# Low parts of some down-projection chunks by an accumulating transfer, with other rates for the modulation rows and fewer idle products at the start

## The chip, the cores and the metric

The kernel runs on one core of a Trainium2 chip, in one launch. The metric is the device time of one execution in microseconds (us); less is better. Each kernel was executed several times, and one execution was recorded by the hardware profiler.

## What is computed

Two layers of an encoder over 512 tokens of width 1024, in float32. Each layer has three sub-layers: a SwiGLU block with 2816 hidden features, a mixer (two attentions, a pooling branch, gates, an output projection), and a second SwiGLU block. Ahead of each stands an RMS norm with a shift and a scale, behind it a gate; these come from a vector `c` through the matrix `w_ada`.

```python
c_act = silu(c)
for l in range(2):
    mod = (c_act @ w_ada[l] + b_ada[l]).reshape(B, 9, 1024)
    h = rms_norm(x, gain[l, 0]) * (1 + mod[:, 1]) + mod[:, 0]
    x = x + 0.5 * mod[:, 2] * ((silu(h @ w_gate) * (h @ w_up)) @ w_down)
    h = rms_norm(x, gain[l, 1]) * (1 + mod[:, 4]) + mod[:, 3]
    x = x + mod[:, 5] * hybrid_mixer(h, ...)
    h = rms_norm(x, gain[l, 2]) * (1 + mod[:, 7]) + mod[:, 6]
    x = x + 0.5 * mod[:, 8] * ((silu(h @ w_gate2) * (h @ w_up2)) @ w_down2)
```

## The kernel before

**Split products.** Every float32 operand is held as two tiles of the rounded type float32r: a high part (the value rounded) and a low part (value minus high part). A product is three matmuls into one PSUM bank, written in `triple` in the order high x high (L119), one factor's low part (L120), the other's (L121). In the down projections (`k_outer`) the weights are the stationary factor, and L121 is the one that needs the weights' low part, `wlo`; L119 and L120 need only the high part, `whi`. With 512 columns these products start some 0.23 us apart.

**Weight chunks.** `wchunk` fetches one chunk of 512 KB: SyncE issues the load into `raw` (two buffers), ScalarE writes the high part (`nc.scalar.copy(hi, raw)`, L272), VectorE the low part (`raw - hi`, L274). `whi` and `wlo` have three buffers each, so the chunk three places on waits until TensorE has finished with this one.

**The four SwiGLU blocks** (class `Ffn`) are counted in the order of the run: the first and second belong to layer 0, the third and fourth to layer 1; a mixer stands between the first and second and between the third and fourth. Each block takes its 22 hidden tiles in four parts of 6, 6, 4 and 6 (`PARTS`). In a part, the gate and up products are made (mostly in pairs by a Winograd-like scheme, `pair`, with weights split by `pair_weights`, which does not go through `wchunk`), and then two passes of `k_outer` multiply with `w_down`, for output columns 0 to 511 (`c0 == 0`, PSUM banks "acc") and 512 to 1023 (`c0 == T`, banks "mm"). A pass has `nf // 2` chunks: three in parts of 6, two in the part of 4. The last two chunks of a pass are held and multiplied output tile by output tile; a chunk ahead of them is multiplied as it comes. In the second pass of parts 0 to 2, and only there, `k_outer` gets a hook `then`, which fetches and splits the next part's first pair of gate weights. Per block these passes have 3 + 3 + 2 = 8 chunks, 32 in all, in 12 passes: 8 long ones (three chunks, of which two are held) and 4 short ones (two, both held), where each output tile takes six products of the first chunk and then six of the second.

**Rows of `w_ada`.** One element of `mod` per partition comes from one 512 KB tile of 128 rows, called a row here: `mod_step` has SyncE load it (L195, into a "v2" buffer, four of them, or a "raw" one) and VectorE multiply and sum it against `silu(c)` (L198). Rows 0 to 15 are taken in the opening, the other 128 in a fixed order from a queue; row counts in the text count these. They are taken in two ways. `side_work`, called for a chunk in `wchunk`, adds a rate to a credit and takes a row for each whole 1, while fewer than `upto` are taken; `ADA_FFN` gives rate and `upto` by layer, block and part. It does nothing for five chunks behind a pass with a norm, nor for chunks that do not go through `wchunk`, nor in a block's last part, where the rest is demanded. `mod_need` takes at once all rows that the next use needs: 8 ahead of part 0's down passes of the first block, 24 ahead of its last part (for the mixer), 72 ahead of the second block's last part, 80 in part 0 of the third, 96 ahead of the third's last part. In the mixers, rows go at a rate of 2.4 up to 56 (first layer) and 128.

**The order of instructions.** The code states what depends on what, a few orders by hand (`issue_after`), and a clock of product counts (`later`, `poll`) by which small work is strewn between the products. The framework fixes each engine's order when the program is built, from the order of the code and the times at which it expects operands and buffers; on the chip each engine then takes its instructions in that order and waits for what isn't there.

**The opening** (`Ffn.start`). Squares of `x` are folded by VectorE in two halves; TensorE sums each half over the partitions (L751). Between them `spin` issues products of constants that nothing reads (L738): `SPIN[0]` beside the first half, `SPIN[1]` beside the second, `SPIN[2]` while VectorE computes the inverse root (from L758), `SPIN[3]` behind the transposes (L768). Each is a float32 product, which the profile shows as two records.

Of the kernel before, what the change touches and what calls it, by code (L numbers as in the profile page):

```python
# [18 lines left out]
AF = mybir.ActivationFunctionType  # L19
ALU = mybir.AluOpType  # L20
# [3 lines left out]
T = 512  # L24
# [16 lines left out]
def encoder_kernel(tc, xT, c, w_ada, b_ada, gains, w_gate, w_up, w_down, w_qkv, w_f, w_ubg,  # L41
                   qk_gain, rel, fbias, w_pool, pool_scale, w_branch, w_out, inv_cnt, w_first, out):
    nc = tc.nc
# [20 lines left out]
    def st(shape, dt, tag, bufs):  # L64
        return sb.tile(shape, dt, tag=tag, bufs=bufs, name=nm(tag))

    def acc(shape=(P, T)):
        return ps.tile(list(shape), F32, tag="acc", bufs=4, name=nm("acc"))

    def mmt(shape=(P, T)):  # L70
        return ps.tile(list(shape), F32, tag="mm", bufs=4, name=nm("mm"))
# [45 lines left out]
    def triple(o, lh, ll, rh, rl, start, stop, onto=False):  # L117
        poll()
        mm(o, lh, rh, start=start, stop=False, skip_group_check=onto)  # L119
        mm(o, lh, rl, start=False, stop=False, skip_group_check=onto)  # L120
        mm(o, ll, rh, start=False, stop=stop, skip_group_check=onto)  # L121
        pe[0] += 3.0 * max(o.shape[-1], 256) / T
# [56 lines left out]
    @contextlib.contextmanager  # L179
    def after(what):  # L180

        if what in last:
            with tc.issue_after(last[what]):
                yield
        else:
            yield
# [47 lines left out]
    @contextlib.contextmanager  # L234
    def behind(engine):

        if engine in gate:
            with tc.issue_after(gate[engine]):
                yield
        else:  # L240
            yield

    def side_work():
        if mod_ptr[0] < flow["upto"]:
            mod_credit[0] += flow["rate"]
        while mod_credit[0] >= 1.0:
            mod_credit[0] -= 1.0
            mod_pop()

    def wchunk(src, shape, side=True, spare=None, lo_eng=None, home=None):  # L250
        if lo_eng is None:
            lo_share[1] += 1
            lo_eng = nc.gpsimd if lo_share[0] and lo_share[1] % lo_share[0] == 0 else nc.vector
        if quiet[0] > 0:
            quiet[0] -= 1
            if quiet[0] == 0:
                gate.clear()
        elif side and flow["on"] and mod_tag[0] == "v2":
            side_work()
        raw = st([P] + list(shape), F32, *(home or (("b", NB) if spare else ("raw", NRAW))))  # L260
        last["dma"] = nc.sync.dma_start(raw, src).ins
        if spare == "ptb":
            both = st([P, 2] + list(shape), F32R, "ptb", 2)
            hi, lo = both[:, 0], both[:, 1]
        elif spare == "b":
            hi = st([P] + list(shape), F32R, "b", NB)
            lo = st([P] + list(shape), F32R, "b", NB)
        else:
            hi = st([P] + list(shape), F32R, "whi", 3)
            lo = st([P] + list(shape), F32R, "wlo", 3)  # L270
        with behind("scalar"):
            nc.scalar.copy(hi, raw)  # L272
        with behind("vector"):
            last["lo"] = lo_eng.tensor_tensor(lo, raw, hi.bitcast(F32), op=ALU.subtract).ins  # L274
        return hi, lo
# [108 lines left out]
    def k_outer(chunk_src, nch, lhs_rhs, before_last=None, bank=None, then=None):  # L384

        if before_last is None:
            parts, nheld = [(None, slice(0, T), [(bank or acc)() for _ in range(4)])], 2
        else:  # L390
            parts = [(hs, slice(hs * HALF, (hs + 1) * HALF), [b((P, HALF)) for _ in range(4)])
                     for hs, b in enumerate((mmt, acc))]
            nheld = 3

        def go(part, j, chunks):
            _, cols, accs = part
            for c, hi, lo in chunks:
                for kk in range(2):
                    a, b, x, y = lhs_rhs(hi[:, kk, :], lo[:, kk, :], 2 * c + kk, j)
                    triple(accs[j], a, b, x[:, cols], y[:, cols], start=(c == 0 and kk == 0),  # L400
                           stop=(c == nch - 1 and kk == 1))

        held = []
        for c in range(nch):
            if before_last is not None:
                if c == nch - 2:
                    quiet[0] = 8
                    before_last()
                quiet[0] = 8
            hi, lo = wchunk(chunk_src(c), (2, T))  # L410
            if c < nch - nheld:
                for part in parts:
                    for j in range(4):
                        go(part, j, [(c, hi, lo)])
            else:
                held.append((c, hi, lo))
        if then is not None:
            then()
        if before_last is not None:
            quiet[0] = 5  # L420
        for part in parts:
            for j in range(4):
                go(part, j, held[:-2])
            for j in range(4):
                go(part, j, held[-2:])
                yield j, part[0], part[2][j]
# [14 lines left out]
    STEP = 3  # L441
    PARTS = (6, 6, 4, 6)
    UP_FROM = 1
    SPIN = (4, 4, 8, 3)


    class Ffn:
# [4 lines left out]
        def gate_up(self, which, n, **kw):  # L452
            return wchunk((w_gate, w_up)[which][self.l, self.s, n], (KD, P), **kw)
# [207 lines left out]
        def run(self, nxt):  # L661
            l, s, ms = self.l, self.s, self.ms
            mod_tag[0] = "v2"
            f0 = 0
            for part, nf in enumerate(PARTS):
                flow.update(on=True, behind="norm", **ADA_FFN(l, s, part))
                acts = []
                n = 0
# [63 lines left out]
        def start(self):  # L732
# [3 lines left out]
            def spin(operands, n):  # L736
                for z in range(n):
                    mm(acc((P, P)), ones, operands[z % len(operands)][:, :P], start=True, stop=True)  # L738
# [4 lines left out]
            for half in range(2):  # L743
# [3 lines left out]
                for tile_ in four[2:]:  # L747
                    fold = nc.vector.tensor_tensor(ssum, ssum, tile_, op=ALU.add)
                spin(four, SPIN[half])
                for t in range(NT):  # L750
                    last["sum"] = mm(pv[:, t:t + 1], ssum[:, t * P:(t + 1) * P], ones[:, 0:1], start=False,  # L751
                                     stop=half == 1, skip_group_check=True).ins
            spin([ssum], SPIN[2])
            gate["vector"] = fold.ins
# [14 lines left out]
            with after("turn"):  # L769
                spin([dg[:, 3, :]], SPIN[3])  # L770
            pgs = [(acc(), acc()), (acc(), acc()), (mmt(), mmt())]
# [29 lines left out]
            for d in range(KD):  # L801
                if d:
                    w = wchunk(w_first[d], (6, P), side=False, lo_eng=nc.gpsimd if d > 1 else nc.vector)
                    h(d)
                else:
                    raw, hi, lo = (st([P, 6, P], z, t, n) for z, t, n in
                                   ((F32, "raw", NRAW), (F32R, "whi", 3), (F32R, "wlo", 3)))
                    last["dma"] = nc.sync.dma_start(raw, w_first[d]).ins
                    nc.scalar.copy(hi, raw)
                    w = hi, lo  # L810
                    h(d, lambda: nc.vector.tensor_tensor(lo, raw, hi.bitcast(F32), op=ALU.subtract).ins)
                product(d, w)
# [384 lines left out]
    class Mixer:  # L1197
# [10 lines left out]
        def run(self, nxt):  # L1208
# [77 lines left out]
            for c0 in (0, T):  # L1286
                def src(c):
                    return w_out[l, 2 * c * P:(2 * c + 2) * P, c0:c0 + T].rearrange("(k p) c -> p k c", p=P)

                def ops(hi, lo, kt, j):  # L1290
                    return (hi[:, j * P:(j + 1) * P], lo[:, j * P:(j + 1) * P], mh[kt][:, 0, :], mh[kt][:, 1, :])

                if c0 == 0:
                    nxt.prefetch("b")
                for j, hs, o in k_outer(src, 4, ops, nxt.prefetch_weights if c0 else None):
                    d = c0 // P + j
                    residual_tail(d, hs, o, modc[:, l, 5, d:d + 1], nxt)
# [3 lines left out]

    def ADA_FFN(l, s, part):
        if l == 0 and s == 0:
            return {"rate": 1.0 if part == 0 else 0.5, "upto": 24}
        if l == 0:
            return {"rate": 0.6, "upto": 80}
        return {"rate": 0.5, "upto": 96}

    LO_SHARE = 0

# [66 lines left out]
```

## Time and profile before

| | us |
|---|---|
| three runs, median (lowest to highest) | 2395.15 (2393.12 to 2395.19) |
| the profiled execution | 2398.11 |
| its span | 2396.3 |
| TensorE busy (matmuls) | 2365.8 |
| VectorE busy | 1783.8 |
| ScalarE busy | 1166.6 |
| GpSimd busy | 196.9 |
| mean granted TensorE clock | 0.997 |

PE is TensorE, PEld its weight loads, DVE VectorE, ACT ScalarE, POOL GpSimd, SP SyncE; SPq and POOLq rows are transfers that they issue. A row of the order of time gives start and duration in us, engine, line, operation, output and inputs, shape, count, and in brackets how long the engine sat idle before and for whom. A row of waits gives the total, the number and the longest. A row of the transfers' list ends with the median time in us from issue to landing.

### The profile page before, as it was taken

To read this page: it belongs to the slowest core of one execution; us is meant where nothing else is said; L and a number is where in the kernel's file an instruction comes from. 1 tells how busy PE (TensorE), PEld (TensorE's weight loads), DVE (VectorE), ACT (ScalarE), POOL (GpSimd) and SP (SyncE) were. 2 spreads that over 40 slices of the span, in tenths; PEclk is the share of its full clock that TensorE was granted. 3 is DMA by queue.
4 is the path that set the end of the run, shared out by engine and by line. 5 is a ranking of instruction groups with operands and counts; after the bars stand their busy time and mean duration, and the time that the engine had idled before them with its cause. 6 is when DMAs were issued, how large, how long until landed. Compare 5 with 4: busy or idle time off the path is not lost. (4 is left out here: it accounts for less than half of the span.)

```text
span 2396.3 us, 36743 instructions
## 1 busy us (share of the span) xinstructions
PE 2365.8 (99%) x14182; PEld 2096.9 (88%) x14182; DVE 1783.8 (74%) x3213; ACT 1166.6 (49%) x2048; POOL 196.9 (8%) x309
## 2 busy tenths in 40 slices
PE   8999999999999999999999999899999999999999
PEld 6899988788888898999998999888888888989998
DVE  7988776687668477778779778776866784777784
ACT  5354445676532353544554445456765334544452
POOL 2000002122220000000100000120221101000000
PEclk9999999999999999999999999999999999999999
DMA  7634342333367414334325423523233773223132
GB/s 275 217 101 134 113 167 98 91 97 119 116 209 280 155 65 167 97 120 145 132 89 194 139 90 115 185 79 99 95 122 116 252 248 132 89 97 123 63 115 89
DMA packets 118484, 325.19 MB, mean 136 GB/s; under 512 B 12034, under 2 KB 14338, under 8 KB 118308
## 3 DMA queue, kind: packets, MB, share of 16 engines
q1 hardware_dynamic: 115106, 314.38, 39.1%
q0 software_dynamic: 3200, 8.46, 1.0%
q8 instruction: 111, 1.82, 0.3%
q14 instruction: 65, 0.53, 0.1%
q10 hardware_dynamic: 2, 0.00, 0.0%
HBM read 316.35 MB, written 6.44 MB: 135 GB/s over the span
## 5 line engine op out<-in xcount | busy, mean ns | idle before, releaser
L272 ACT CAST whi<-raw 128x1024 fp32r<-128x1024 f32 (+1 forms) x260 | 270.4, 1044 | 336.7 <-PE acc L120 193.0
L274 DVE TENSOR_TENSOR wlo<-raw,whi 128x1024 fp32r<-128x1024 f32 (+1 forms) x254 | 311.5, 1230 | 142.2 <-ACT whi L272 140.3
L121 PE MATMUL acc<-b,wlo 128*128 128x512 f32 (+1 forms) x704 | 261.8, 373 | 8.4 <-DVE wlo L274 8.4
L119 PE MATMUL acc<-b,whi 128*128 128x512 f32 (+1 forms) x704 | 262.6, 375 | 1.1 <-ACT b L380 1.1
L120 PE MATMUL acc<-b,whi 128*128 128x512 f32 (+1 forms) x704 | 261.5, 372 | 1.2 <-DVE b L381 1.2
L121 PE MATMUL mm<-b,wlo 128*128 128x256 f32 (+1 forms) x768 | 245.8, 320 | 2.0 <-DVE wlo L274 1.9
L119 PE MATMUL mm<-b,whi 128*128 128x256 f32 (+1 forms) x768 | 245.1, 319 | 0.2 <-ACT t L583 0.2
L120 PE MATMUL mm<-b,whi 128*128 128x256 f32 (+1 forms) x768 | 245.2, 319 | 0.0
L198 DVE CUSTOM_DVE_ANT_0 v<-v,b,badac 128x1024 f32<-128x1024 f32 x144 | 186.8, 1306 | 26.8 <-DMA v<-in_w_ada_dram 26.6
L119 PE MATMUL mm<-hhi,whi 128*128 128x256 f32 (+1 forms) x616 | 199.1, 324 | 1.1 <-ACT t L583 1.0
L121 PE MATMUL mm<-hhi,wlo 128*128 128x256 f32 (+1 forms) x616 | 199.1, 323 | 0.5 <-DVE wlo L274 0.5
L120 PE MATMUL mm<-hlo,whi 128*128 128x256 f32 (+1 forms) x616 | 199.1, 323 | 0.0
L120 PE MATMUL acc<-hlo,whi 128*128 128x512 f32 x480 | 188.1, 392 | 1.7 <-DVE hlo L787 1.6
L119 PE MATMUL acc<-hhi,whi 128*128 128x512 f32 x480 | 188.0, 396 | 1.6 <-ACT hhi L784 1.6
L121 PE MATMUL acc<-hhi,wlo 128*128 128x512 f32 x480 | 187.6, 391 | 0.0
L380 ACT CAST whi<-raw 128x1024 fp32r<-128x1024 f32 x96 | 100.6, 1048 | 132.9 <-PE mm L120 79.0
L121 PEld LDWEIGHTS acc<-b,wlo 128*128 128x128 f32 x704 | 133.5, 190 | 32.6 <-DVE wlo L274 9.7
L121 PEld LDWEIGHTS mm<-b,wlo 128*128 128x128 f32 x768 | 147.1, 192 | 13.4 <-DVE wlo L274 3.5
L119 PEld LDWEIGHTS mm<-b,whi 128*128 128x128 f32 x768 | 147.0, 191 | 10.4 <-ACT t L583 0.4
L120 PEld LDWEIGHTS mm<-b,whi 128*128 128x128 f32 x768 | 147.0, 191 | 10.2
L120 PEld LDWEIGHTS acc<-b,whi 128*128 128x128 f32 x704 | 133.4, 190 | 24.6 <-DVE b L381 2.7
L119 PEld LDWEIGHTS acc<-b,whi 128*128 128x128 f32 x704 | 133.4, 190 | 24.3 <-ACT b L380 2.8
(326 smaller groups left out, 6119.0 us busy)
## 6 DMA issues: line engine op xcount, KB each, us to landing
v<-in_w_ada_dram SPq DMA_DIRECT2D x144, 512.0 KB, 5.0
raw<-in_w_down_dram SPq DMA_DIRECT2D x88, 512.0 KB, 3.8
raw<-in_w_up_dram SPq DMA_DIRECT2D x82, 512.0 KB, 3.6
b<-in_w_gate_dram SPq DMA_DIRECT2D x76, 512.0 KB, 6.2
raw<-in_w_ubg_dram SPq DMA_DIRECT2D x56, 512.0 KB, 3.6
raw<-in_w_qkv_dram SPq DMA_DIRECT2D x42, 512.0 KB, 4.0
raw<-in_w_branch_dram SPq DMA_DIRECT2D x24, 512.0 KB, 3.9
raw<-in_w_out_dram SPq DMA_DIRECT2D x16, 512.0 KB, 3.6
```

Of the source, the lines that this page charges most:

```text
L119: mm(o, lh, rh, start=start, stop=False, skip_group_check=onto)
L120: mm(o, lh, rl, start=False, stop=False, skip_group_check=onto)
L121: mm(o, ll, rh, start=False, stop=stop, skip_group_check=onto)
L198: dot = nc.vector.tensor_tensor_reduce(out=raw, in0=raw, in1=silc[0], scale=1.0, scalar=badac[:, l, j, d:d + 1], op0=ALU.mult, op1=ALU.add ...
L272: nc.scalar.copy(hi, raw)
L274: last["lo"] = lo_eng.tensor_tensor(lo, raw, hi.bitcast(F32), op=ALU.subtract).ins
L380: nc.scalar.copy(hi, src)
```

## The change

For the 32 chunks of the passes that have the hook `then`, ScalarE writes a negated copy of the raw tile into the low part's tile (rounded as the high part is), and a transfer of GpSimd's queue reads the same weights again from memory and adds them to it, so the tile holds raw minus high part as before. The rates of the rows change in all blocks. In the opening, four idle products beside the second half and one of the eight behind it are left out.

```diff
-    def wchunk(src, shape, side=True, spare=None, lo_eng=None, home=None):
+    def wchunk(src, shape, side=True, spare=None, lo_eng=None, home=None, by_dma=False):
...
         with behind("scalar"):
             nc.scalar.copy(hi, raw)
+        if by_dma:
+            with behind("scalar"):
+                nc.scalar.activation(lo, raw, AF.Copy, scale=-1.0)
+            nc.gpsimd.dma_start(lo, src, accum_op=ALU.add, max_dma_last_dim=2048)
+            return hi, lo
         with behind("vector"):
             last["lo"] = lo_eng.tensor_tensor(lo, raw, hi.bitcast(F32), op=ALU.subtract).ins
         return hi, lo
...
-            hi, lo = wchunk(chunk_src(c), (2, T))
+            hi, lo = wchunk(chunk_src(c), (2, T), by_dma=then is not None)
...
-    SPIN = (4, 4, 8, 3)
+    SPIN = (4, 0, 7, 3)
...
     def ADA_FFN(l, s, part):
         if l == 0 and s == 0:
-            return {"rate": 1.0 if part == 0 else 0.5, "upto": 24}
+            return {"rate": 0.7 if part == 0 else 1.25, "upto": 24}
         if l == 0:
-            return {"rate": 0.6, "upto": 80}
-        return {"rate": 0.5, "upto": 96}
+            return {"rate": 1.0, "upto": 80}
+        return {"rate": 0.7, "upto": 96}
```

## The prediction

> **What bounds the kernel now.** I read the page's head first, then TensorE's waits, then the order of time around the longest of them, and last the stretches in which the change acts.
>
> ```profile
> span 2396.3 us, 36743 instructions
> PE 2365.8 (99%) x14182; PEld 2096.9 (88%) x14182; DVE 1783.8 (74%) x3213; ACT 1166.6 (49%) x2048; POOL 196.9 (8%) x309
> ```
>
> TensorE works in 2365.8 of 2396.3 us. No product is removed but a few idle ones at the start, so nothing beyond its 30.5 us of idle time, and the time it runs at a lower clock, can be won. The waits say what is worth looking at:
>
> ```profile
> PE acc L121 <- DVE wlo L274: 8.4, 3, 5.1
> ```
>
> Three waits for a low part hold 8.4 us. TensorE's order of time shows them:
>
> ```profile
> 346.19 0.39 PE L120 MATMUL acc<-b,whi 128*128 128x512 f32 x1
> 349.52 0.80 PE L121 MATMUL acc<-b,wlo 128*128 128x512 f32 x1 [2.94 <-DVE wlo L274]
> ...
> 1177.83 0.50 PE L121 MATMUL acc<-b,wlo 128*128 128x512 f32 x1 [0.43 <-DVE wlo L274]
> ...
> 1531.13 0.39 PE L121 MATMUL acc<-b,wlo 128*128 128x512 f32 x1
> 1536.59 0.80 PE L121 MATMUL acc<-b,wlo 128*128 128x512 f32 x1 [5.08 <-DVE wlo L274]
> ```
>
> Each is the first down pass of a block's last part, just behind a heap of w_ada rows, which the next block needs. SyncE's order of time shows the heaps: 4 + 1 rows, 4 rows, 4 + 3 + 1 rows.
>
> ```profile
> 327.74 9.11 SPq L195 DMA_DIRECT2D v<-in_w_ada_dram  x4
> 339.61 0.33 SPq L195 DMA_DIRECT2D v<-in_w_ada_dram  x1
> ...
> 1158.56 8.90 SPq L195 DMA_DIRECT2D v<-in_w_ada_dram  x4
> ...
> 1509.16 9.50 SPq L195 DMA_DIRECT2D v<-in_w_ada_dram  x4
> 1521.61 3.86 SPq L195 DMA_DIRECT2D v<-in_w_ada_dram  x3
> 1528.43 0.33 SPq L195 DMA_DIRECT2D v<-in_w_ada_dram  x1
> ```
>
> A stall costs more than its wait, since the clock falls behind it, after 2.94 us of idleness already. Busy times by stretch (from, to and length, then the engines, then the granted clock, DMA share and GB/s):
>
> ```profile
> 349.00:353.00 4.00, 3.48 (x9) 2.77 (x10) 4.00 (x5) 3.25 (x4) 0.00 (x0) 0.57 1.02 367
> 1526.00:1536.00 10.00, 5.52 (x25) 4.21 (x23) 8.64 (x21) 3.32 (x7) 0.00 (x0) 0.88 0.93 326
> 1536.00:1546.00 10.00, 9.41 (x39) 7.88 (x40) 8.37 (x9) 8.12 (x11) 4.00 (x3) 0.78 0.54 195
> 1546.00:1556.00 10.00, 8.06 (x53) 7.66 (x52) 5.90 (x7) 2.88 (x6) 3.22 (x4) 0.83 0.49 157
> ```
>
> At 0.57 for 4 us, 4 x 0.43 = 1.7 us are lost. The products stand 3.33 us apart over the first stall where 0.23 is usual, so it costs 3.1 + 1.7 = 4.8 us. The second: 5.46 - 0.23 = 5.2, and 1.2 + 2.2 + 1.7 = 5.1 by the three clocks, so 10.3 us. The one at 1177.83 costs 0.6.
>
> **The rates.** A rate is added at each weight chunk loaded in a block's parts, and a row is taken for each whole 1. Counting with the code: the first block issues 8 + 4 rows in part 0 as now 14, then 7 as now 3, and 5 as now 2; that makes 24, all the mixer needs, and its heap of 5 is gone. The second block has 18 chunks that count: 18 rows as now 11, so it stands at 74 where 72 are needed, and its heap of 4 is gone. The third block reaches 80 by its own demand in part 0 (5 rows at once as now 7), then 16 x 0.7 and what was left over make 11 where 16 x 0.5 made 8: its heap shrinks from 8 to 5. I price a heap of 5 at the 4.8 us of the first block's. Gain: 4.8 + 0.6 + (10.3 - 4.8) = 10.9 us.
>
> The rows don't vanish:
>
> ```profile
> L198 DVE CUSTOM_DVE_ANT_0 v<-v,b,badac 128x1024 f32<-128x1024 f32 x144 | 186.8, 1306 | 26.8 <-DMA v<-in_w_ada_dram 26.6
> ```
>
> 1.31 us of VectorE each, 4 more in part 1 and 3 more in part 2 of the first block, 7 more in the second. I cost them at nothing: what hides them is that the low parts of these parts' chunks leave VectorE (below). If that cover fails, a row that waits for its load holds back whatever low part is queued behind it, by up to the 1.5 us (26.6 us in 18 waits) that such a wait takes.
>
> **The opening.**
>
> ```profile
> 9.73 1.49 DVE L748 TENSOR_TENSOR t<-t,wlo 128x512 f32<-128x512 f32 x2
> ...
> 14.42 0.16 DVE L758 TENSOR_SCALAR nt_v<-mm 128x4 f32<-128x4 f32 x1 [2.00 <-PE mm L751]
> ```
>
> TensorE's weight loads there:
>
> ```profile
> 10.76 1.83 PEld L738 LDWEIGHTS acc<-wlo,ones 128*128 128x128 f32 x8
> 12.47 1.83 PEld L751 LDWEIGHTS mm<-ones,t 128*128 128x128 f32 x8
> ```
>
> The second sum of squares is ready at 9.73 + 1.49 = 11.22, but its products wait behind the four idle products (eight records) from 10.76 until 12.47, and VectorE waits for them. Without those they start at about 11.3: -1.2 us for the whole chain. The product less behind them (8 to 7) leaves the transposes no later. Bounds: -1.2, and zero if the clock then rises later.
>
> **The low parts of 32 chunks.** Removed: 32 subtractions on VectorE. Added: 32 negated copies on ScalarE, 32 issues on GpSimd's queue, 32 more reads of 512 KB.
>
> ```profile
> L274 DVE TENSOR_TENSOR wlo<-raw,whi 128x1024 fp32r<-128x1024 f32 (+1 forms) x254 | 311.5, 1230 | 142.2 <-ACT whi L272 140.3
> ```
>
> Two of the stages, by stretch:
>
> ```profile
> 200.00:217.00 17.00, 17.00 (x79) 14.15 (x79) 12.22 (x16) 4.72 (x5) 0.00 (x0) 1.00 0.32 93
> 268.00:279.00 11.00, 11.00 (x50) 9.13 (x49) 10.97 (x15) 3.65 (x5) 0.00 (x0) 1.00 0.16 50
> ```
>
> VectorE gives back 32 x 1.23 = 39 us, worth nothing by itself: in these stages TensorE is full (17.00 of 17.00, 11.00 of 11.00). ScalarE takes 32 copies, by its rows below 1.05 us each, 34 us, where it works 4.72 of 17 and 3.65 of 11; GpSimd is idle there. The price lies in the landing, which the low product waits for:
>
> ```profile
> x_dram<-xv POOLq DMA_DIRECT2D x8, 512.0 KB, 3.1
> raw<-in_w_down_dram SPq DMA_DIRECT2D x88, 512.0 KB, 3.8
> b<-in_w_gate_dram SPq DMA_DIRECT2D x76, 512.0 KB, 6.2
> q1 hardware_dynamic: 115106, 314.38, 39.1%
> ```
>
> No accumulating transfer is in the trace. Its nearest row is GpSimd's own of the same size, 3.1 us; the far end is two loads in turn, 2 x 3.8 = 7.6. Queue q1 moved 314 MB in 39.1% of the span, 1.56 us for 512 KB; a second stream read (the destination's) adds that: 3.1 + 1.6 to 3.8 + 1.6, so I take 5.0.
>
> The Trainium skill (DMA: Bandwidth & Descriptors, Anatomy of one DMA - SWDGE (gpsimd) path) gives a GpSimd transfer 2.0 us and its bytes at 436 GB/s, 3.2 us for 512 KB, to which the row of 3.1 agrees. By it, with the destination's bytes counted too, the landing would be an estimated 4.4 us, and the first rival below would stand at 2411 instead of its 2418.
>
> What room is there? Chunks of a part's second pass get their buffer when the first pass ends. ScalarE's high part and TensorE's first low product of the last chunk, in a part of two chunks
>
> ```profile
> 266.84 1.05 ACT L272 CAST whi<-raw 128x1024 fp32r<-128x1024 f32 x1 [1.61 <-PE acc L120]
> ```
>
> ```profile
> 270.00 0.39 PE L121 MATMUL mm<-b,wlo 128*128 128x512 f32 x1
> ```
>
> and, in a part of three chunks,
>
> ```profile
> 201.78 1.04 ACT L272 CAST whi<-raw 128x1024 fp32r<-128x1024 f32 x1
> ```
>
> ```profile
> 207.31 0.39 PE L121 MATMUL mm<-b,wlo 128*128 128x512 f32 x1
> ```
>
> In the first the negated copy would end at 266.84 + 2 x 1.05 = 268.94: 1.1 us before the need. In the other at 203.9, so 3.4 before. With 5.0 us of landing the written order stalls 3.9 us in each of the 4 short stages and 1.6 in each of the 8 long ones, 28.4 us, and 4 x 1.7 for the clock: 35. But TensorE's order isn't the written one where a low part is late:
>
> ```profile
> 114.03 0.39 PE L119 MATMUL mm<-b,whi 128*128 128x512 f32 x1
> 114.26 0.43 PE L121 MATMUL mm<-b,wlo 128*128 128x512 f32 x1
> ```
>
> As written, L121 always follows L120 of its own step; here another step's L119 runs ahead of it. The order is fixed when the program is built, by when operands are expected. A short stage can put all 24 products of its first chunk ahead of the second's low ones: 18 more, and with them the other six high ones of the second, 24 x 0.227 = 5.4 us; the room becomes 1.1 + 5.4 = 6.5, over 5.0. So I take no whole stall, only misjudged landings. The nearest measure is the rows above: 26.6 us over 144 loads, 0.185 each; 20 of the 32 chunks are tight (two in each long stage, one in each short): 20 x 0.185 = 3.7 us. Bounds: 0 and, at 7.6 us in the written order, 4 x 6.5 + 8 x 4.2 = 60 and clock.
>
> The sum: -10.9 - 1.2 + 3.7 = -8.4 on the profiled execution's 2398.11 us (span 2396.3, 1.8 around it): 2389.7. The median shown, 2395.15, lies 2.96 lower, so 2386.7; say 2387.
>
> **Rivals.** *The landing sets the pace* (slower). The loads that SyncE issues start when ScalarE has read a raw tile, at the very moment the accumulating transfer is issued; with several in flight w_gate's loads take 6.2 us instead of 3.8. If the order is built for an early landing, the stalls are those of the written order: at 5.0 us 35 - 12.1 = +23, 2418. It decides from a landing of about 4 us, where 4 x 2.9 + 8 x 0.6 = 16.4 passes the 12.1 won. For it: the room of 1.1 us; against: the bent order. The Trainium skill (DMA: Bandwidth & Descriptors, Issuing engines are not separate DMA queues) speaks for it: GpSimd's transfers interleave with SyncE's on the same engines. Chance 0.34.
>
> *A draw*: landings misjudged by 1 us in each of the 12 stages eat the 12.1 won, 2395; or the heap of 5 in the third block costs as much as that of 8 did, and what is left is 4.8 + 0.6 + 1.2 - 3.7 = 2.9, 2392. Together 0.18.
>
> *All covered*: no landing shows, and the last heap's stall goes too: -12.1 - 4.8, 2378; 0.10.
>
> **How the numbers follow.** My forecast, 2381 to 2392 by itself, has 0.38. About 0.2% (4.8 us) is what a measurement can tell from no change. Faster: 0.38 + 0.10 = 0.48; same 0.18; slower 0.34. The range runs from 2380, which leaves out part of the best case, to 2425, past the first rival's 2418, which leaves out landings over 5.5 us in the written order (12 x 0.5 = 6 us more).
>
> **What would show it.** Right: no wait of TensorE behind a heap near 346, the wait near 1531 down to some 3 us, none of more than 1 us for a GpSimd transfer, and products in the second passes with high ones ahead of low ones. Wrong: TensorE waits of 2 to 5 us for the wlo transfers, twelve times, clocks of 0.5 behind them, or a landing over 6 us; or waits for L274 at other chunks, where the rows went.

## The result, and the profile after

The changed kernel takes 2479.98 us (median of four, 2477.35 to 2484.53), the kernel before in the same session 2395.17 (2393.12 to 2397.11): a ratio of 1.0358, 95% interval 1.0343 to 1.0374. It is 85 us slower, where 8 us of gain were forecast. The profiled execution has a span of 2482.8 us, 86.5 more than before, and a mean granted clock of 0.986 against 0.997.

The page's head and its busy times first; in the changed kernel `wchunk`'s negated copy stands in L275, the accumulating transfer in L276 and VectorE's low part in L279.

```profile
span 2482.8 us, 36848 instructions
...
PE 2394.1 (96%) x14172; PEld 2108.6 (85%) x14172; DVE 1751.1 (71%) x3181; ACT 1196.1 (48%) x2080; POOL 233.0 (9%) x341
```

VectorE's busy time fell by 33 us and ScalarE's rose by 30, near the 39 and 34 that the count of operations gave, and neither engine is full. TensorE's idle time, the span less its busy time, rose from 30.5 to 88.7 us. Its waits say for what (total, times, longest):

```profile
PE mm L121 <- DMA wlo<-in_w_down_dram: 61.2, 25, 6.5
...
PE acc L121 <- DVE wlo L279: 3.9, 2, 2.6
```

The waits for VectorE's low parts in the first down passes are 3.9 us where they were 8.4; 2.6 of them stand behind the third block's heap of rows. In their place TensorE waits 61.2 us, in 25 places, for the accumulating transfers. The page's list of transfers and the answer for L276 (from issue to landing: shortest, median, longest) give the reason:

```profile
wlo<-in_w_down_dram POOLq DMA_DIRECT2D x32, 512.0 KB, 10.1
```

```profile
DMA to landing us min/median/max: 6.8/10.1/11.9
```

Even the shortest is over the 5.0 us that the prediction took. One short pass shows how it acts. ScalarE, GpSimd's issues and TensorE, in order of time:

```profile
291.32 1.05 ACT L272 CAST whi<-raw 128x1024 fp32r<-128x1024 f32 x1 [4.47 <-PE acc L120]
292.28 1.06 ACT L275 ACTIVATE wlo<-raw 128x1024 fp32r<-128x1024 f32 x1
```

```profile
283.90 1.19 POOL L276 DMA_DIRECT2D wlo<-in_w_down_dram  x1 [65.75 <-ACT b L385]
293.63 1.20 POOL L276 DMA_DIRECT2D wlo<-in_w_down_dram  x1 [8.55 <-ACT wlo L275]
```

```profile
292.66 0.39 PE L119 MATMUL mm<-b,whi 128*128 128x512 f32 x1
292.89 0.39 PE L120 MATMUL mm<-b,whi 128*128 128x512 f32 x1
295.04 0.50 PE L121 MATMUL mm<-b,wlo 128*128 128x512 f32 x1 [1.76 <-DMA wlo<-in_w_down_dram]
...
298.57 0.39 PE L120 MATMUL mm<-b,whi 128*128 128x512 f32 x1
301.35 0.50 PE L121 MATMUL mm<-b,wlo 128*128 128x512 f32 x1 [2.39 <-DMA wlo<-in_w_down_dram]
```

The first chunk's transfer, issued at 283.90 with some 9 us to spare, isn't there at the third product of the pass; the second chunk's, issued at 293.63, is missed again behind the product of 298.57. The order is bent a little (between the two waits some high products of the second chunk run early), but L121 still stands right behind the first two products. In all eight long passes the whole order is the written one. By stretch, one short pass and one long:

```profile
292.00:306.00 14.00, 9.86 (x42) 7.53 (x41) 9.39 (x13) 4.68 (x6) 1.20 (x1) 1.00 0.48 102
1063.00:1084.00 21.00, 15.06 (x52) 11.33 (x51) 10.88 (x14) 7.45 (x8) 2.37 (x2) 0.84 0.64 151
```

TensorE works 9.86 of 14 us and 15.06 of 21, where such passes were full before. In the long one the granted clock is 0.84 behind the waits, while in the short one it stays at 1.00. Over the span the two mean clocks leave (1 - 0.986) x 2482.8 = 35 us lost against 7 before, 28 more. TensorE's busy time shows the same 28 us (2394.1 against 2365.8, with ten records fewer), and its idle time 58: the 61 us of waits, less what was won at the heaps, with some smaller waits. Together they make the 86.5.

### The profile page after: what moved, and what is told of

It reads as the page before. It is cut to its first block, busy times and chain, and to the rows that moved or that the text cites. A ratio compares the mean times of both kernels' runs of the same rounds, so it can differ in the third digit from the quotient of the medians.

```text
span 2482.8 us, 36848 instructions
## 1 busy us (share of the span) xinstructions
PE 2394.1 (96%) x14172; PEld 2108.6 (85%) x14172; DVE 1751.1 (71%) x3181; ACT 1196.1 (48%) x2080; POOL 233.0 (9%) x341
## 5 line engine op out<-in xcount | busy, mean ns | idle before, releaser
L279 DVE TENSOR_TENSOR wlo<-raw,whi 128x1024 fp32r<-128x1024 f32 (+1 forms) x222 | 271.4, 1226 | 137.8 <-ACT whi L272 135.9
L121 PE MATMUL mm<-b,wlo 128*128 128x256 f32 (+1 forms) x768 | 257.9, 338 | 61.5 <-DMA wlo<-in_w_down_dram 61.2
L121 PE MATMUL acc<-b,wlo 128*128 128x512 f32 (+1 forms) x704 | 261.0, 371 | 3.9 <-DVE wlo L279 3.9
L119 PE MATMUL mm<-b,whi 128*128 128x256 f32 (+1 forms) x768 | 254.5, 331 | 1.1 <-ACT whi L272 1.1
L120 PE MATMUL mm<-b,whi 128*128 128x256 f32 (+1 forms) x768 | 254.0, 331 | 0.0
L121 PEld LDWEIGHTS mm<-b,wlo 128*128 128x128 f32 x768 | 152.4, 198 | 86.6 <-DMA wlo<-in_w_down_dram 74.7
L121 PE MATMUL mm<-hhi,wlo 128*128 128x256 f32 (+1 forms) x616 | 199.0, 323 | 0.0
L121 PE MATMUL acc<-hhi,wlo 128*128 128x512 f32 x480 | 187.6, 391 | 0.0
L119 PEld LDWEIGHTS mm<-b,whi 128*128 128x128 f32 x768 | 152.6, 199 | 12.6 <-ACT whi L272 1.6
L120 PEld LDWEIGHTS mm<-b,whi 128*128 128x128 f32 x768 | 152.1, 198 | 12.9
L121 PEld LDWEIGHTS acc<-b,wlo 128*128 128x128 f32 x704 | 133.0, 189 | 27.2 <-DVE wlo L279 4.6
## 6 DMA issues: line engine op xcount, KB each, us to landing
wlo<-in_w_down_dram POOLq DMA_DIRECT2D x32, 512.0 KB, 10.1
```

## The experiments

All times stand beside runs of the kernel before on the same chip; these had medians of 2395 to 2397 us. Theory L says that the landing of the transfers makes the whole loss, waits and clock, and that the rates and the opening win what was forecast. Rival R says that the rows at the new rates cost a part of it.

**The parts by themselves.**

e1_no_dma: all of the change but the transfers.

```diff
-            hi, lo = wchunk(chunk_src(c), (2, T), by_dma=then is not None)
+            hi, lo = wchunk(chunk_src(c), (2, T), by_dma=False)
```

> The changed kernel with its low parts made by VectorE again; rates and opening stay changed. Theory L (the landing of the accumulating transfers, 10.1 us median, costs 61 us of waits and 27 us of lower clock, and the rates and the opening win about 9 us): 2383 to 2389 us, no wait of TensorE over 3.5 us. Rival R (the rows at the new rates crowd VectorE and cost a part of the 85 us by themselves): over 2400 us, with TensorE waits for L274's low parts in the middle parts.

2384.48 us, ratio 0.9950 (0.9934 to 0.9966). TensorE's two longest waits in total:

```profile
PE mm L145 <- ACT b L133: 3.7, 1, 3.7
PE acc L119 <- ACT b L385: 2.6, 2, 1.3
```

and SyncE's rows ahead of the third block's last part:

```profile
1502.95 8.06 SPq L195 DMA_DIRECT2D v<-in_w_ada_dram  x4
1513.76 0.33 SPq L195 DMA_DIRECT2D v<-in_w_ada_dram  x1
```

A heap of 4 + 1 rows is left there, as counted; it causes no wait, and the mean clock is 1.000. Theory L holds, R falls.

e2_dma_only: the kernel before with the transfers alone (rates and `SPIN` as before).

> The kernel before with only the accumulating transfers. Theory L: the whole loss and more, as the rates' gain is missing: 2483 to 2495 us, transfers landing in about 10 us, the heap stalls near 346 and 1531 still there. Rival R: under 2475 us.

2485.47 us, ratio 1.0380 (1.0359 to 1.0400); the waits are those of both kernels at once:

```profile
PE mm L121 <- DMA wlo<-in_w_down_dram: 62.4, 24, 5.7
PE acc L121 <- DVE wlo L279: 9.5, 3, 4.9
```

e3_rates_only: the kernel before with the new `ADA_FFN`.

> The kernel before with only the new rates of the rows. Theory L, with the prediction's count of the heaps: -8 to -11 us, 2384 to 2388. Rival R: the rows need the room that the transfers give VectorE, so without it the gain is eaten: 2393 us or more.

2386.00 us, ratio 0.9961 (0.9946 to 0.9975). The rows need no help from the transfers.

e4_spin_only: the kernel before with `SPIN = (4, 0, 7, 3)`.

> The kernel before with only the five idle products left out in the opening. Prediction: VectorE's nt_v (14.42 us before) at about 13.2 and everything behind it 1.2 us earlier: 2393 to 2395 us, no difference that the runs can tell. Rival: the clock rises a window later, and the first products give the 1.2 us back or lose more.

2391.94 us, ratio 0.9982 (0.9973 to 0.9992). VectorE's step behind the second sum, which started at 14.42 us before:

```profile
13.04 0.16 DVE L758 TENSOR_SCALAR nt_v<-mm 128x4 f32<-128x4 f32 x1 [0.67 <-PE mm L751]
```

1.4 us earlier, and the first down product follows 1.5 us earlier (89.89 against 91.35). The runs say 4 us (2 to 6); the trace shows only these 1.5, and what the rest would be stays open.

**The transfer.** The next four vary it inside the changed kernel.

e5_plain_copy: no adding. The 32 low parts are then the weights themselves.

```diff
-            with behind("scalar"):
-                nc.scalar.activation(lo, raw, AF.Copy, scale=-1.0)
-            nc.gpsimd.dma_start(lo, src, accum_op=ALU.add, max_dma_last_dim=2048)
+            nc.gpsimd.dma_start(lo, src, max_dma_last_dim=2048)
```

> The changed kernel, but GpSimd's transfer only copies the weights into the low part's tile: no adding and no negated copy by ScalarE. The low parts of the 32 chunks are then the weights themselves. Theory A (the adding makes the landing long, since the destination is read too): landing 4 to 5 us, waits for it under 10 us in total, about 2390 to 2400 us. Rival D (GpSimd writes 256 descriptors of 2 KB, and that takes the time): landing still 7 us or more, waits of 30 us or more.

```profile
wlo<-in_w_down_dram POOLq DMA_DIRECT2D x32, 512.0 KB, 5.6
```

Landing 5.6 us, waits of 10.6 in 9 places, 2402.56 us, ratio 1.0035 (1.0023 to 1.0047). The copy also starts sooner, since nothing negates ahead of it: a pass's first one 10 to 13.5 us ahead of the pass, where the adding one had 7 to 10, and none of these first ones is waited for. In this kernel a transfer that adds takes nearly twice as long as a copy (alone the two are closer, below), though even the copy of a later chunk is waited for.

e6_rows_4k laid `w_down` out so that a chunk's row is one run of 4 KB; f1_rows_4k also raised the limit on a piece:

```diff
-    r["w_down"] = a["ffn_w_down"]
+    r["w_down"] = a["ffn_w_down"].reshape(L, 2, KF // 2, 2, P, 2, T).transpose(0, 1, 2, 5, 4, 3, 6)
...
-            nc.gpsimd.dma_start(lo, src, accum_op=ALU.add, max_dma_last_dim=2048)
+            nc.gpsimd.dma_start(lo, src, accum_op=ALU.add, max_dma_last_dim=4096)
```

> The changed kernel with w_down laid out so that a chunk's row for a partition is one run of 4 KB; the accumulating transfer then needs 128 descriptors in place of 256. Rival D: landing falls from 10.1 to 6 us or less, waits from 61 to 15 us or less. Theory A: landing stays at 9 us or more.

> As e6_rows_4k, whose transfers were still cut into 256 pieces of 2 KB, now with pieces of 4 KB: 128 descriptors. Theory D (the number of descriptors sets the landing): 6 us or less, waits under 20 us, under 2415 us. If not the number: landing 9 us or more and 2470 us.

e6 told nothing of the number of pieces: its transfers still went out as 256 pieces of 2 KB, landing 10.0 us, 2475.93 us, ratio 1.0344 (1.0321 to 1.0366). With 128 pieces of 4 KB (f1) the landing is 9.0 us, waits 53.0, 2470.72 us, ratio 1.0313 (1.0294 to 1.0331): a tenth shorter, so the number of pieces is not the main cause.

e7_from_sbuf: the same addition with the source on the chip (`nc.gpsimd.dma_start(lo, raw, accum_op=...)`).

> The changed kernel, but the accumulating transfer reads the raw tile on the chip in place of the weights in memory. If reading memory beside the loads of SyncE made it slow: landing under 7 us. Theories A and D: 9 us or more; the raw tile is then held until the transfer has landed, so the next load starts later and the stalls grow.

```profile
wlo<-raw POOLq DMA_DIRECT2D x32, 512.0 KB, 6.6
```

6.6 us, waits of 45.3, 2457.63 us, ratio 1.0267 (1.0239 to 1.0296). Under 7, as if memory were the cause; but the raw tile is now held while the transfer runs, so SyncE's load into it does not start with it. The two had to be parted.

e8_first_only: the transfer only for the first chunk of each pass (`by_dma=then is not None and c == 0`).

> The changed kernel with the accumulating transfer only for the first chunk of each of the 12 passes (the chunk with some 9 us of room behind its negated copy), the other 20 low parts by VectorE again. Theory L, room counted against a landing that is shorter without a second transfer right behind: waits of 0 to 2 us per pass, 2385 to 2405 us. If any transfer on GpSimd's queue hurts whatever its room: waits of 2 us or more in most passes, over 2415 us.

Landing 10.7 us with no second transfer behind it, waits of 17.9 in 9 places, 2414.93 us, ratio 1.0085 (1.0065 to 1.0104). Neither side's number: room of 9 us is too little for 10.7, and the length doesn't come from two transfers in a row. The packet records of this run say what goes with it: the two transfers beside which SyncE's queue moved at most 1.2 MB in the first 6 us landed in 7.1 and 7.8 us, the other ten, beside 1.3 to 2.1 MB, in 8.6 to 11.8.

**The landing by itself.** m1_landing computes nothing; it issues single transfers, each waiting for the one ahead (its negated copy reads that one's tile), with loads that start when ScalarE has read their tiles, as in the kernel. Shortened, one transfer is:

```python
nc.scalar.activation(lo, prev, AF.Copy, scale=-1.0)
nc.scalar.activation(lo, loads[0], AF.Copy, scale=-1.0)   # with loads only
nc.gpsimd.dma_start(lo, down(n), accum_op=ALU.add, max_dma_last_dim=2048)
for z in loads[:nload]:
    nc.sync.dma_start(z, down(n + 3))
```

> Nothing is computed here: the kernel only times single transfers of 512 KB on GpSimd's queue, four of each kind, each waiting for the one ahead: a plain copy, an accumulating one from memory, one whose source lies on the chip, one with 128 rows of 4 KB, one beside one load of SyncE's and beside four, and one beside eight VectorE operations. Theory S (the accumulating transfer is slow by itself): 8 us or more alone, 10 beside the others. Rival B (what runs beside it makes it slow): 5 to 7 us alone, 9 or more beside the four loads or beside VectorE, and the row that rises names the cause.

```profile
plain<-in_w_down_dram POOLq DMA_DIRECT2D x4, 512.0 KB, 4.3
alone<-in_w_down_dram POOLq DMA_DIRECT2D x4, 512.0 KB, 5.6
fromsbuf<-still POOLq DMA_DIRECT2D x4, 512.0 KB, 5.0
rows4k<-in_w_gate_dram POOLq DMA_DIRECT2D x4, 512.0 KB, 5.4
oneload<-in_w_down_dram POOLq DMA_DIRECT2D x4, 512.0 KB, 8.0
fourload<-in_w_down_dram POOLq DMA_DIRECT2D x4, 512.0 KB, 8.9
vector<-in_w_down_dram POOLq DMA_DIRECT2D x4, 512.0 KB, 5.9
```

Alone an accumulating transfer lands in 5.6 us. VectorE beside it adds 0.3 and one load 2.4. Two of these rows mix cases, as the issues and landings of single transfers show. Of the four in `fourload`, two had only one load beside them and took 7.9 us; the two that had four took 9.9 and 11.1. Of the four in `plain`, two ran beside loads of the opening; the two that did not took 4.1. Rival B, what runs beside it, is right.

g1_hold_raw keeps the raw tile taken until the landing, with memory as the source:

```diff
             nc.gpsimd.dma_start(lo, src, accum_op=ALU.add, max_dma_last_dim=2048)
+            held = st([P, 16], F32, "hd", 1)
+            nc.gpsimd.tensor_tensor(held, raw[:, 0, :16], lo[:, 0, :16].bitcast(F32), op=ALU.add)
```

> The changed kernel with one small GpSimd addition behind each accumulating transfer, which reads the raw tile and the landed low part: the raw tile stays taken until the landing, so no load can start at the moment of the transfer. Its cost is that a part's last transfer is issued only after the one ahead has landed. Theory B (the load that SyncE starts at that moment makes the landing long): landing 6 to 7.5 us. If other work does it: 9 us or more.

Landing 7.5 us at the median (5.7 to 10.5), waits of 57.9, one run of 2470.88 us. The landing falls as theory B said, to the edge of its range; loads into other tiles (`w_gate`'s) still run beside it. The time hardly falls. Ten of the twelve first chunks are not waited for, where it was two, but a long pass's third chunk is now loaded into the raw tile that was held: in the pass at 206 us its load is issued at 207.71, right behind the addition that frees the tile, and its transfer only at 214.30, 5.8 us behind the second chunk's, where the changed kernel has 1.9.

g2_beside repeats the measurement with a run of twelve loads, for three kinds.

> Only single transfers again, four of each kind: a plain copy, an accumulating one from memory and one from the chip; each alone, beside one load issued at the same moment, and beside a run of twelve loads. Theory Q (the share of the engines decides): each kind gets longer by about what the load moves, 1.5 us for one. Theory O (GpSimd's transfer starts late and its packets fall behind the load's): +2.4 us for all three kinds beside one load, and 10 us or more for the accumulating one beside the run. If reading memory is what suffers, the kind from the chip stays near 5.0.

```profile
plain_one<-in_w_down_dram POOLq DMA_DIRECT2D x4, 512.0 KB, 4.8
alone_one<-in_w_down_dram POOLq DMA_DIRECT2D x4, 512.0 KB, 8.0
fromsbuf_one<-still POOLq DMA_DIRECT2D x4, 512.0 KB, 6.3
plain_run<-in_w_down_dram POOLq DMA_DIRECT2D x4, 512.0 KB, 8.3
alone_run<-in_w_down_dram POOLq DMA_DIRECT2D x4, 512.0 KB, 11.1
fromsbuf_run<-still POOLq DMA_DIRECT2D x4, 512.0 KB, 11.4
```

(In this kernel SyncE issued some of the later loads early, beside the kinds that were to be alone, so those values are taken from m1_landing.) No theory has all of it. Beside one load a copy takes 0.7 us longer than the 4.1 alone, an addition from the chip 1.3 and one from memory 2.4; beside the run a copy needs 8.3 and both additions need 11 us, so the source no longer matters. The kernel's 10.1 lies where a transfer beside several loads lies.

**The order.** f2_low_last writes the 12 passes with all high products first.

```diff
+        if then is not None:
+            chunks = [(c, *wchunk(chunk_src(c), (2, T), by_dma=True)) for c in range(nch)]
+            then()
...
+            for low in (False, True):
+                for c, hi, lo in chunks:
...
```

> The changed kernel with the 12 passes written so that all high products of all chunks come first and the products with the low parts last. The prediction held that the order has the room for a late landing; the changed kernel's order did not use it. With it, the last chunk of a long pass has 14.5 us from the pass's start instead of 7.3, the second of a short one 9.1 instead of 1.8: at 10 us of landing no stall in long passes and about 2 us in the short ones: 8 us of waits, 2390 to 2400 us. If the landing grows when the order gives it room, or the four output tiles that now end together stall what follows: over 2420 us.

2396.82 us, ratio 1.0001 (0.9992 to 1.0010): 83 us of the 85 are gone, with the landing as long as ever. The transfer's row, TensorE's wait for it (L419 is the low product here), and a short pass from 273.6 us on:

```profile
wlo<-in_w_down_dram POOLq DMA_DIRECT2D x32, 512.0 KB, 9.6
```

```profile
PE mm L419 <- DMA wlo<-in_w_down_dram: 3.2, 3, 2.0
```

```profile
280.66 0.39 PE L422 MATMUL mm<-b,whi 128*128 128x512 f32 x1
280.89 1.30 PE L419 MATMUL mm<-b,wlo 128*128 128x512 f32 x5
```

The first low product comes 7.3 us into the pass, behind 32 high ones, and waits for nothing.

g3_low_last_dve: the same order, low parts by VectorE (`by_dma=False` in that line).

> f2_low_last without its transfers: the same order in the 12 passes, the low parts made by VectorE. Theory: the order costs nothing and what f2 lies above e1_no_dma (12 us) is the transfers' own, so 2383 to 2387 us. Rival: the order costs it (four output tiles end together): 2393 to 2398 us.

2383.87 us, ratio 0.9946 (0.9925 to 0.9967). The order costs nothing; the 13 us that f2 lies above it belong to the transfers and their negated copies. The two profiled spans differ by 10.3 us (2395.7 and 2385.4): TensorE is idle for 5.1 us more in f2, of which 3.2 are its waits for transfers and 1.4 a high part that ScalarE makes later (2.6 against 1.2), and busy for 5.2 us more, with half the clock over 10.2 us at two waits where g3 has 3.4. The third block's heap stalls in both, 3.2 and 2.8 us.

f3_rate_1: e1_no_dma with a rate of 1.0 in layer 1.

> e1_no_dma (rates and opening changed, low parts by VectorE) with a rate of 1.0 in place of 0.7 in layer 1, so that by the count of rows no heap is left in the third block. Theory L: the heap of 5 there costs e1 at most 1.5 us (its one gap over 1.3 us near 1431 aside), so 2382 to 2385, hardly to be told from e1. If more rows in the middle parts crowd VectorE: 2387 or more.

2380.98 us, ratio 0.9943 (0.9931 to 0.9956). The last heap was worth nothing that can be told from e1. Both beat both kernels: the change without its transfers is the version to keep.

## Why the prediction was wrong, point by point

- *The rates, -10.9 us.* Right: by themselves they give -9.3 (e3), and with the opening -12.0 (e1, both by the ratios), where the forecast's two terms make -12.1. The count of rows held (heaps of 0 and 5). The price of a heap of 5 differs from kernel to kernel: 4.8 us was taken; the changed kernel and g3 have a wait of 2.6 and 2.8 us behind it, and half the clock for 3.4 us (1.7 lost); e1 shows no wait there.
- *The cover for the extra rows.* The prediction made it hang on the low parts that leave VectorE. That was not needed: e3 has the rows without it.
- *The opening, -1.2 us.* Right in its mechanism, 1.4 us in the trace of e4.
- *VectorE's 39 us and ScalarE's 34 cost and bring nothing.* The first part is right: f2 has this relief of VectorE and g3 has not, and f2 is the slower. What the copies cost is part of the 13 us between the two and was not tried alone.
- *A landing of 5.0 us.* The first step that failed. For a transfer alone it was close (5.6 in m1), and so was the way there: adding costs 1.5 us over a copy, where 1.6 was taken, and the copy takes 4.1, where 3.1 to 3.8 was. But in the kernel loads of SyncE run beside every one: 10.1 us. The prediction knew the reason, named it in its first rival (loads start at the very moment that the transfer is issued, and w_gate's rows show 6.2 us for 3.8), and left it out of the sum.
- *"So I take no whole stall, only misjudged landings"*, 3.7 us. The step that failed with it: 61.2 us of waits where 3.7 was taken. The high products could have covered the landing: f2, with the low products written last, puts the second chunk's need in a short pass 9.1 us behind its start instead of the written order's 1.8, and a landing of 9.6 us then costs 3.2 us of waits. But the order of the changed kernel does not do so. One bent stretch near 114 us, where VectorE was late, was taken as proof that the order would bend as far as it had to; the changed kernel's order does not: in 10 of the 12 passes the first chunk's L121, whose transfer had some 9 us, stands third and is waited for. These first chunks, which the prediction did not count among its tight ones, make 17 us of the 61. That the order was built with an earlier landing in mind is likely, but was not tried.
- *Neither step alone makes the loss.* With a landing of 5.6 us (e5, whose copies also start earlier) the kernel lies some 20 us above e1, by the ratios; with the landing left long and the order written for it (f2), 12. Together they lose 98.
- *The slower rival* named the mechanism: landing sets the pace, in the written order. Its price, 2418, used 5.0 us. With 10.1 and the prediction's own rooms, 4 x (10.1 - 1.1) + 8 x (10.1 - 3.4) = 90 us of waits would come out; measured are 61, likely because a wait for one chunk moves the need of the next and because short passes are bent a little. The upper bound of the landing, 7.6 us, was itself too low: it put two loads in turn, and no row for a transfer that competes.

The Trainium skill (DMA: Bandwidth & Descriptors, Issuing engines are not separate DMA queues) says that transfers of all issuing engines run on the same DMA engines and interleave. The runs agree, and add the size: 2.4 us for one load beside an accumulating transfer, 5.5 for a run of them. The estimate of 4.4 us worked out from the bytes per second of that page of the Trainium skill is under what even a lone transfer takes.

## What to carry to other kernels

A transfer's time in a busy kernel is its time beside the loads that the same event sets free, not its time alone: look at which tile its start releases, and who fills it. Before a low-priority operand is moved to something slower, ask where its consumer stands in the order that is built, and write the order so that the late operand is used last; an order that bent once for one lateness is no promise for another. And test the parts of a bundled change one by one: here two of three were worth 12 us and hid behind the third, which by itself cost 90.

## What the runs showed of the hardware

The packets of the accumulating transfer don't slow down when it has company; they come later. In the packet records each 2 KB piece takes 0.176 to 0.178 us, alone (m1) as in the kernel. Alone the first piece starts 1.9 us after the issue and the last ends at 5.3; beside one load issued at the same moment 2.5 and 7.6; beside a run (g2) 4.8 to 5.8 and 10.0 to 11.6; in the kernel, for the first chunk of a pass, 2.5 to 5.1 and 6.5 to 11.2. So beside a run some 3.5 us are lost ahead of the first piece and 2 between the pieces. What holds them back wasn't tried. A copy has pieces of 0.099 us. The limit on a piece counts bytes: 2048 cut rows of 4 KB in two (e6).
